# The mixer's values as one block of 1024 columns, with seven products for three of its pairs, and pool's grouped product and all heads behind it

## The chip, the cores and the metric

The kernel runs on one core of a Trainium2 chip. Its time is the device time of one execution in microseconds, as the median of the runs. The engines are named as in the profile: PE (products), PEld (its weight loads), DVE (vector engine), ACT (scalar engine with function tables), POOL, and SP, which issues the DMAs.

## The reference

One layer of an encoder for 256 frames of 2048 channels in f32: a SwiGLU half step, a mixer, cross attention to 256 memory tokens, a second SwiGLU half step, and a last norm. The change lies in the mixer:

```python
h = rms_norm(x, mix_norm[l])
proj = h @ w_in[l]
u, q, k, v, g, a_lr = jnp.split(proj, list(IN_SPLITS), axis=-1)   # 1024, 512, 512, 1024, 1024, 16 columns
y_pool = pool_mixer(u, pool_w[l], pool_scale[l])      # 4 groups: causal means, then a 256 x 256 product each
y_gla = gla_mixer(q, k, v, g, a_lr, ...)              # 4 heads of 128 (q, k) and 256 (v) channels
x = x + jnp.concatenate([y_pool, y_gla], axis=-1) @ w_out[l]
```

In `gla_mixer` each head's scores (256 x 256, causal by chunks of 64 frames, with a decay by channel of k) are multiplied with its values; the result is normed by head and gated with silu(g).

## The kernel before

Everything lies in SBUF with channels on the partitions: `xs` and `ys` hold 16 tiles of 128 channels, each with a high and a low part of 256 frames, which together give nearly f32 precision. Weights stream in one unit of 1 MB after the other. `Stream` holds the units in order: each has a load (a DMA from SP into one of three `raw` buffers), a split into a high part (ACT's cast, `wh`) and a low part (DVE's difference, `wl`), and a function that issues its products. A unit is split two units before its products; `wh` and `wl` have three buffers, so a split waits until PE has read the unit three before it. Operations between the units (`st.op(f, n)`) are put into the stream n units later. A scheduler of the language then settles each engine's own order by its own estimate; an engine then works strictly in that order.

PSUM has four tiles of two banks (`ptile`), which all products share in turn.

The units of the mixer, in order, with the short names used below: two blocks for pool's u (8 units); the low-rank unit; q (4 units); k (k1 to k4); the pool unit (`pool_unit`, 48 products of 256 columns for the four grouped 256 x 256 products, from the pooled inputs that lie in tiles 8 to 15 of `ys`); v (v1 to v8); the gate g (g1 to g8). u, q, k and g are made by `block_a`, with channels on the partitions (32 products a unit, tiles named pa). The values are made by `block_b` as two blocks of 512 columns with frames on the partitions: v1 to v4, then v5 to v8, 24 products of 512 columns a unit (tile pb).

A head goes through these steps: `scores` (ACT's and DVE's factors into a tile QD, named m in the trace; the products pq; DVE's copies into the single tile ST), `attend` (the products po; ACT's square, DVE's copy) and `head_squares` (DVE). For two heads together, `head_norms` adds squares over channels on PE (pn) and takes the root (`rsqrt`: DVE, ACT's square root, DVE, then four diagonal tiles), and `head_scale` spreads the factors over the partitions (PE, ps) and multiplies the heads' tiles on DVE. `ev_g` evicts a gate tile: ACT's copy and DVE's sum, silu, the product with the head's tile, and the split into `ys` tiles 8 to 15, over the pooled inputs. `pool_out` writes pool's results into `ys` tiles 0 to 7.

The heads stood like this: scores of heads 0 and 1 behind v5 and v6, the others behind v8 and g1, `head_norms` behind g1 and g3, `head_scale` behind g2 and g5, each then placed among the products by the scheduler.

Elsewhere the kernel has a cheaper block already, `block_s`: one block of 1024 columns with frames on the partitions, in which chosen units ("sevens") do a 2 x 2 product of blocks with seven products in place of eight, that is 21 instructions in place of 24. A seven needs four sums of `xs` blocks (`Sums.make`: five small DVE operations, then a cast and a difference), a longer split (`split_seven`: three sums of weights into T, high and low parts xh and xl of the weights, and wh and wl of T), four PSUM tiles, and at its end a combination (`combine`) and two joins (`join`) on DVE. The tables `OUT_HOMES` and the like say which tiles lend T, xh and xl their room.

Of the kernel before, what the change touches and what calls it, by code (L numbers as in the profile page):

```python
# [9 lines left out]
AF = mybir.ActivationFunctionType  # L10
# [4 lines left out]
P = 128  # L15
D = 2048
S = 256
# [3 lines left out]
NB = 512  # L21
CH = 64
H = 4
# [76 lines left out]
def build(ctx, tc, I, out):  # L100
    nc = tc.nc
    st = Stream()
# [9 lines left out]
    def open_scope(name, shared=None):  # L112


        def f():
            scope["shared"] = shared or {}
            scope["stack"] = ExitStack()
            scope["pool"] = scope["stack"].enter_context(
                tc.tile_pool(name=name, bufs=1, reuse_waits="tile")
            )  # L120
        return f
# [203 lines left out]
    def block_a(srcs, act, evict, delays=(0, 1)):  # L325

        n_k = 4 * len(srcs)
        held = {}

        def unit(gi):  # L330
            def fn(wh, wl):
                if gi == 0:
                    held["ps"] = [ptile(uid("pa")) for _ in range(2)]
                wh, wl = (w.rearrange("p (k n) -> p k n", n=NB) for w in (wh, wl))
                for kk in range(4):
                    k = 4 * gi + kk
                    last = k == n_k - 1
                    a = act[:, k]
                    for n in range(4):
                        ps = held["ps"][n // 2][:, n % 2, :]  # L340
                        cols = slice(n * P, (n + 1) * P)
                        parts = [(ps, wh[:, kk, cols], a.rearrange("p a b -> p (a b)")),
                                 (ps[:, S:], wl[:, kk, cols], a[:, 0, :])]
                        if last:
                            parts.reverse()
                        for i, (o, w, x) in enumerate(parts):
                            nc.tensor.matmul(  # L347
                                o, w, x, start=k == 0 and i == 0, stop=last and i == 1
                            )
            return fn  # L350

        for gi, src in enumerate(srcs):
            st.unit(src, unit(gi))
        for p in range(2):
            st.op(lambda p=p: evict(p, held["ps"][p]), delays[p])
# [48 lines left out]
    class Sums:  # L404
# [1 line left out]

        def __init__(self, name, act, pairs, over, room):
            self.name, self.act, self.pairs, self.over = name, act, pairs, over  # L410
            self.room, self.where = room, {}

        def make(self, g):
            act, i = self.act, self.pairs.index(g)
            n = 3 if self.over else 4
            if i == 0 or i >= self.room:
                room, tag = (self.room, self.name) if i == 0 else (1, f"{self.name}{i}")
                t = scope["pool"].tile([P, room * 6 * P], F32R, tag=tag, name=uid(tag))
                held = min(len(self.pairs), self.room) if i == 0 else 1
                t = t[:, : held * 2 * n * P].rearrange("p (g a n s) -> p g a n s", a=2, n=n, s=P)  # L420
                self.where.update({i + k: t[:, k] for k in range(held)})
            own = self.where[i]
            a, k = jtile(), slice(2 * g, 2 * g + 2)
            nc.vector.tensor_tensor(
                out=a.rearrange("p (k s) -> p k s", k=2), in0=f32(act[:, k, 0, :]),
                in1=f32(act[:, k, 1, :]), op=ALU.add,
            )

            a = a.rearrange("p (n s) -> p n s", n=4)
            p11, p21, p12, p22 = (a[:, m] for m in range(4))  # L430
            nc.vector.tensor_tensor(out=p11, in0=p11, in1=p21, op=ALU.subtract)
            nc.vector.tensor_tensor(out=p21, in0=p22, in1=p21, op=ALU.subtract)
            nc.vector.scalar_tensor_tensor(
                out=p22, in0=p11, scalar=-1.0, in1=p22, op0=ALU.mult, op1=ALU.subtract
            )
            added = nc.vector.tensor_tensor(out=p12, in0=p12, in1=p22, op=ALU.add)
            split(own[:, 0], own[:, 1], a[:, 4 - n :])
            if self.over:
                split(act[:, 2 * g, 0, P:], act[:, 2 * g, 1, P:], p11)
            return None, added  # L440
# [164 lines left out]
    def block_b(srcs, act, evict, delay=0):  # L605

        n_k = 4 * len(srcs)
        held = {}

        def unit(gi):  # L610
            def fn(wh, wl):
                if gi == 0:
                    held["ps"] = ptile(uid("pb"))
                wh, wl = (w.rearrange("p (k n) -> p k n", n=NB) for w in (wh, wl))
                for kk in range(4):
                    k = 4 * gi + kk
                    for h in range(2):
                        products(held["ps"][:, h, :], act, k, h, wh[:, kk], wl[:, kk],
                                 k == 0, k == n_k - 1)
            return fn  # L620

        for gi, src in enumerate(srcs):
            st.unit(src, unit(gi))
        st.op(lambda: evict(held["ps"]), delay)
# [6 lines left out]
    def wblock(w, n0, k0=0, nk=KT):  # L631

        def src(k):
            return lambda raw: wload(raw.rearrange("p (k n) -> p k n", n=NB), w, k, 4, n0)
        return [src(k0 + k) for k in range(0, nk, 4)]
# [301 lines left out]
    ffn(I["ffn1_w_gate"][0], I["ffn1_w_up"][0], I["ffn1_w_down"][0], down_first,  # L937
        amid_first)
    st.op(close_scope, 1)
    st.op(open_scope("s_mix"), 1)  # L940


    w_in = I["w_in"][0]
# [2 lines left out]
    def mt(name, shape, tag=None, bufs=1):  # L946
        t = whole_lines(scope["pool"], shape, F32, tag or name, uid(name), bufs)
        mix[name] = t
        return t
# [68 lines left out]
    def pool_out(g):  # L1018
        for dt in range(2):
            split_scaled(ys, 2 * g + dt, mix["pp", g][:, dt, :], gcol(G_PS + 2 * g + dt))  # L1020
# [88 lines left out]
    st.op(ev_a)  # L1109
    st.op(decay, 2)  # L1110
    block_a(wblock(w_in, 2 * NB), xs, ev_q)
    block_a(wblock(w_in, 3 * NB), xs, ev_k)
    st.unit(load_pool, pool_unit)
    for g in range(4):
        st.op(lambda g=g: pool_out(g))

    def ev_v(b):
        def evict(ps):
            if b == 0:
                mt("v", [P, 2, 2 * NB])  # L1120
                s = mt("ST", [P, 2, S])
                nc.gpsimd.memset(s[64:128, 0, 0:CH], 0.0)
                nc.gpsimd.memset(s[64:128, 1, 2 * CH : 3 * CH], 0.0)
            for h in range(2):
                nc.scalar.activation(
                    mix["v"][:, h, b * NB : (b + 1) * NB], ps[:, h, :], AF.Copy, scale=Rcol[:, h : h + 1]
                )
        return evict

    def scores(h):  # L1130
        q, kd, E, F = mix["q"][:, h, :], mix["k"][:, h, :], mix["E"], mix["F"]
# [22 lines left out]
            nc.vector.tensor_copy(s[part, j // 2, j * CH :], ps[part, j // 2, j * CH : S])  # L1154

    def attend(h):
        s, v = mix["ST"], mix["v"]
        po = ptile(uid("po"))
        for vt in range(2):
            col = h * DV + vt * P  # L1160
            nc.tensor.matmul(  # L1161
                po[:, vt, :S], v[:, 0, col : col + P], s[:, 0, :], start=True, stop=False
            )
            nc.tensor.matmul(
                po[:, vt, 2 * CH : S], v[:, 1, col : col + P], s[:, 1, 2 * CH :], start=False, stop=True
            )
        if h % 2 == 0:
            mix["oz", h // 2] = as_four(m4())
        q = mix["osq", h] = ttile()
        nc.scalar.activation(q, po[:, :, :S], AF.Square)  # L1170
        i = h % 2
        nc.vector.tensor_copy(mix["oz", h // 2][:, 2 * i : 2 * i + 2, :], po[:, :, :S])

    def head_squares(h):
        sq = mix["osq", h]
        nc.vector.tensor_tensor(out=sq[:, 0, :], in0=sq[:, 0, :], in1=sq[:, 1, :], op=ALU.add)
# [14 lines left out]
    def head_scale(b):  # L1191
        ps = ptile(uid("ps"))
        for i in range(4):
            spread(ps[:, i // 2, :], i % 2, mix["diag"][i])
        for i in range(2):
            oz = mix["oz", b][:, 2 * i : 2 * i + 2, :]
            nc.vector.tensor_tensor(out=oz, in0=oz, in1=bc(ps[:, i, :S]), op=ALU.mult)
# [12 lines left out]
            split_pair(ys, 8 + 2 * h, t)  # L1210
        return evict

    for b in range(2):
        block_b(wblock(w_in, (4 + b) * NB), xs, ev_v(b))
        for i in range(2):
            h = 2 * b + i
            at = 1 + i - b
            st.op(lambda h=h: scores(h), at)
            st.op(lambda h=h: attend(h), at + 1)
            st.op(lambda h=h: head_squares(h), at + 1)  # L1220
        st.op(lambda b=b: head_norms(b), 5 - 2 * b)
        st.op(lambda b=b: head_scale(b), 6 - b)
    block_a(wblock(w_in, 6 * NB), xs, ev_g(0), (0, 0))
    block_a(wblock(w_in, 7 * NB), xs, ev_g(1))
    st.op(close_scope, 1)
# [401 lines left out]
```

## Time and profile before

| | |
|---|---|
| median of 3 runs | 2081.63 us (2081.42 to 2082.89) |
| the profiled execution: its own time | 2082.5 us |
| its span, first to last instruction | 2080.3 us |
| mean granted clock of TensorE | 0.999 |

A matmul's row shows how long it was under way; matmuls overlap, so that the distance of two starts is what one costs. In the rows, x counts instructions, and a bracket at the end of a timeline's row tells how long the engine had been idle and what ended that. Times in the views by time are microseconds from the span's start. f32 products that aren't split (pq, po, pn, ps) appear as two records each.

### The profile page before, as it was taken

How to read it: one execution, taken by the hardware profiler on the slowest of the kernel's cores; microseconds unless marked ns; L12 is line 12 of the kernel's file. 1: busy time of each engine (PE TensorE's matmuls, PEld its weight loads, DVE VectorE, ACT ScalarE, POOL GpSimd, SP SyncE). 2: the span in 40 equal slices, each digit the busy share in tenths (PEclk: the TensorE clock that was granted, in tenths of full speed). 3: DMA queues.
4: the chain of work that ended last, by engine and by line, in shares of the span. 5: the costliest groups of instructions: out<-in, count | busy, mean ns of one | idle time of the engine just before them, and what ended most of it. 6: DMA issues, size and time to landing. Idle time of an engine off the chain costs nothing.

```text
span 2080.3 us, 24347 instructions
## 1 busy us (share of the span) xinstructions
PE 2067.9 (99%) x9651; PEld 1726.1 (83%) x9651; DVE 1800.3 (87%) x1686; ACT 1143.5 (55%) x1136; POOL 98.6 (5%) x87
## 2 busy tenths in 40 slices
PE   9999999999999999999999999999999999999998
PEld 7888888888888888888888888888888888888886
DVE  6998899989998677579889878879988999889987
ACT  7664455544555545455656554656554555545554
POOL 0000000000000000000000000000100010000001
PEclk9999999999999999999999999999999999999999
DMA  7666766566656755557655555666576765676664
GB/s 264 203 202 223 242 216 214 187 229 228 234 194 220 247 180 182 162 182 266 224 180 194 168 182 182 204 221 204 181 243 215 235 209 191 224 241 223 210 226 151
DMA packets 131178, 435.95 MB, mean 210 GB/s; under 512 B 9844, under 2 KB 13528, under 8 KB 130680
## 3 DMA queue, kind: packets, MB, share of 16 engines
q1 hardware_dynamic: 130888, 433.86, 61.9%
q8 instruction: 76, 1.25, 0.2%
q10 hardware_dynamic: 176, 0.53, 0.1%
q14 instruction: 38, 0.31, 0.0%
HBM read 417.58 MB, written 16.78 MB: 209 GB/s over the span
## 4 chain that ended last, share of the span: by engine, by line
PE 99%; DMA 0%; DVE 0%; ACT 0%; SPq 0%; DVEq 0%; issue 0%; ACTq 0%
PE pt L362 58%; PE pt L507 28%; PE pa L347 7%; PE pb L362 2%; PE ph L780 1%; PE pl L1321 1%; PE pv L1358 1%; PE px L791 1%; DMA x<-in_x 0%; PE pp L1012 0%; PE pe L362 0%; PE pa L1039 0%; PE po L1161 0%; PE tm L1268 0%; PE px L717 0%; PE pq L1148 0%
## 5 line engine op out<-in xcount | busy, mean ns | idle before, releaser
L362 PE MATMUL pt<-wh,xs 128*128 128x512 f32 x2080 | 667.5, 390 | 0.0
L453 DVE TENSOR_TENSOR wl<-raw,wh 128x2048 fp32r<-128x2048 f32 (+1 forms) x253 | 545.2, 2161 | 133.2 <-ACT wh L1585 132.9
L1585 ACT CAST wh<-raw 128x2048 fp32r<-128x2048 f32 x253 | 483.2, 1912 | 295.3 <-PE pt L362 134.2
L362 PE MATMUL pt<-wh,ys 128*128 128x512 f32 x1472 | 464.0, 389 | 0.0
L489 ACT CAST wh<-T 128x1024 fp32r<-128x1024 f32 x242 | 254.1, 1055 | 368.5 <-DVE T L486 358.8
L362 PEld LDWEIGHTS pt<-wh,xs 128*128 128x128 f32 x2080 | 389.6, 188 | 80.2 <-ACT wh L1585 0.2
L362 PE MATMUL pt<-wl,xs 128*128 128x512 f32 x1040 | 405.5, 391 | 0.0
L362 PEld LDWEIGHTS pt<-wh,ys 128*128 128x128 f32 x1472 | 276.2, 188 | 57.1
L362 PE MATMUL pt<-wl,ys 128*128 128x512 f32 x736 | 286.9, 390 | 0.0
L453 DVE TENSOR_TENSOR wl<-T,wh 128x2048 fp32r<-128x2048 f32 (+1 forms) x121 | 271.6, 2245 | 2.5 <-ACT wh L489 2.2
L362 PEld LDWEIGHTS pt<-wl,xs 128*128 128x128 f32 x1040 | 195.3, 188 | 39.8
L280 DVE TENSOR_TENSOR xl<-raw,xh 128x1536 fp32r<-128x1536 f32 x121 | 211.9, 1751 | 13.5 <-ACT xh L279 13.4
L279 ACT CAST xh<-raw 128x1536 fp32r<-128x1536 f32 x121 | 179.0, 1480 | 49.8 <-PE pt L507 31.3
L486 DVE TENSOR_TENSOR T<-T,raw 128x512 f32<-128x512 f32 x242 | 167.0, 690 | 6.3
L362 PEld LDWEIGHTS pt<-wl,ys 128*128 128x128 f32 x736 | 138.2, 188 | 28.4
L486 DVE TENSOR_TENSOR T<-raw 128x1024 f32<-128x1024 f32 x121 | 147.4, 1219 | 0.5
L507 PE MATMUL pt<-wh,xs 128*128 128x512 f32 x376 | 146.2, 389 | 0.0
L507 PE MATMUL pt<-xh,xs 128*128 128x512 f32 x376 | 140.3, 389 | 0.0
L457 POOL TENSOR_TENSOR wl<-raw,wh 128x768 fp32r<-128x768 f32 x40 | 74.2, 1856 | 1373.9 <-DVE wl L453 1351.1
L347 PE MATMUL pa<-xs,wh 128*128 128x512 f32 x384 | 135.6, 397 | 0.0
L507 PE MATMUL pt<-wh,xe 128*128 128x512 f32 x320 | 124.4, 389 | 0.0
L347 PE MATMUL pa<-xs,wl 128*128 128x256 f32 x384 | 106.8, 282 | 0.0
(248 smaller groups left out, 2343.9 us busy)
## 6 DMA issues: line engine op xcount, KB each, us to landing
raw<-in_ffn_w_down SPq DMA_DIRECT2D x88, 1024.0 KB, 5.6
raw<-in_ffn_w_up SPq DMA_DIRECT2D x80, 1024.0 KB, 5.0
raw<-in_ffn_w_gate SPq DMA_DIRECT2D x77, 1024.0 KB, 5.1
raw<-in_w_in SPq DMA_DIRECT2D x32, 1024.0 KB, 5.2
raw<-in_xattn_w_kv SPq DMA_DIRECT2D x32, 1024.0 KB, 5.0
raw<-in_w_out SPq DMA_DIRECT2D x16, 1024.0 KB, 5.5
raw<-in_xattn_w_q SPq DMA_DIRECT2D x16, 1024.0 KB, 5.5
raw<-in_xattn_w_o SPq DMA_DIRECT2D x16, 1024.0 KB, 6.0
```

What stands on the lines that cost most here:

```text
L279: in_turn("scalar", lambda: nc.scalar.copy(hi, src))
L280: in_turn("vector", lambda: nc.vector.tensor_tensor(out=lo, in0=src, in1=f32(hi), op=ALU.subtract))
L347: nc.tensor.matmul(o, w, x, start=k == 0 and i == 0, stop=last and i == 1)
L362: nc.tensor.matmul(ps, a, w, start=first and i == 0, stop=last and i == 2)
L453: in_turn("vector", lambda: nc.vector.tensor_tensor(out=lo[:, :n], in0=src[:, :n], in1=f32(hi[:, :n]), op=ALU.subtract))
L457: rest = nc.gpsimd.tensor_tensor(out=lo[:, n:], in0=src[:, n:], in1=f32(hi[:, n:]), op=ALU.subtract)
L486: in_turn("vector", lambda: nc.vector.tensor_tensor(out=o, in0=a, in1=b, op=ALU.add))
L489: in_turn("scalar", lambda: nc.scalar.copy(th[:, c], t[:, c]))
L507: nc.tensor.matmul(banks[n], x, w, start=n in fresh and j == 0, stop=n in ends and j == 2)
L780: nc.tensor.transpose(v[:, i, h * P : (h + 1) * P], g[:, h, i * P : (i + 1) * P], ident)
L791: nc.tensor.transpose(v[:, j, h * P : (h + 1) * P], x[:, h, j * P : (j + 1) * P], ident)
L1585: in_turn("scalar", lambda: nc.scalar.copy(hi, raw))
```

## The change

The values become one `block_s` of 1024 columns: units v1 to v8 load 256 rows of 1024 columns each, and pairs 2, 4 and 6, at places 3, 5 and 7 (v3, v5, v7), are sevens. Their sums (`v_sums`) are made in the k block (put 0, 1 and 2 units behind the q block) and lie in tiles 0 to 5 of `ys`, which are free until `pool_out`; so `Sums` takes places from outside. T, xh and xl get one tile each in the mixer's scope (`MIX_HOMES`; xh and xl have two elsewhere). The values now lie in the tile that the combination writes; ACT scales them there, and `v_part` finds a head's columns. The pool unit and `pool_out` move from behind the k block to behind v8. ST takes the room of the low-rank weights (wa2). All four heads follow the pool unit: scores of head h behind the pool unit and h gate units, `attend` and `head_squares` one unit later, `head_norms` behind g3 and g5, `head_scale` behind g4 and g6. The gate blocks themselves stay as they are.

```diff
-        def __init__(self, name, act, pairs, over, room):
+        def __init__(self, name, act, pairs, over, room, where=None):
             self.name, self.act, self.pairs, self.over = name, act, pairs, over
-            self.room, self.where = room, {}
+            self.room, self.where, self.own = room, where or {}, where is None
...
-            if i == 0 or i >= self.room:
+            if self.own and (i == 0 or i >= self.room):
...
-    st.op(open_scope("s_mix"), 1)
+    MIX_HOMES = {"T": [("T", D, 1)], "xh": [("xh", 3 * NB, 1)], "xl": [("xl", 3 * NB, 1)]}
+    st.op(open_scope("s_mix", MIX_HOMES), 1)
...
     block_a(wblock(w_in, 2 * NB), xs, ev_q)
+    def in_ys(i):
+        t = ys[:, 2 * i : 2 * i + 2].rearrange("p k a s -> p (k a s)")
+        return t.rearrange("p (a n s) -> p a n s", a=2, n=4)
+
+    v_sums = Sums("ve", xs, (2, 4, 6), False, 3, {i: in_ys(i) for i in range(3)})
+    for g, after in zip(v_sums.pairs, (0, 1, 2)):
+        st.op(lambda g=g: among_weights(lambda: v_sums.make(g)), after)
     block_a(wblock(w_in, 3 * NB), xs, ev_k)
-    st.unit(load_pool, pool_unit)
-    for g in range(4):
-        st.op(lambda g=g: pool_out(g))
-
-    def ev_v(b):
-        def evict(ps):
-            if b == 0:
-                mt("v", [P, 2, 2 * NB])
-                s = mt("ST", [P, 2, S])
...
+    def v_home():
+        return mt("v", [P, 4, NB])
+
+    def ev_v(j, c):
+        for h in range(2):
+            nc.scalar.activation(c[:, h, :], c[:, h, :], AF.Copy, scale=Rcol[:, h : h + 1])
+
+    def v_part(t, col):
+        j, at = divmod(col, NB)
+        return mix["v"][:, 2 * (1 - j) + t, at : at + P]
+
+    def score_tile():
+        s = mt("ST", [P, 2, S], "wa2")
...
-    for b in range(2):
-        block_b(wblock(w_in, (4 + b) * NB), xs, ev_v(b))
-        for i in range(2):
-            h = 2 * b + i
-            at = 1 + i - b
-            st.op(lambda h=h: scores(h), at)
-            st.op(lambda h=h: attend(h), at + 1)
-            st.op(lambda h=h: head_squares(h), at + 1)
-        st.op(lambda b=b: head_norms(b), 5 - 2 * b)
-        st.op(lambda b=b: head_scale(b), 6 - b)
+    block_s(wwide(w_in, 4 * NB), xs, v_sums, tuple(range(8)), ev_v, home=v_home)
+    st.unit(load_pool, pool_unit)
+    for g in range(4):
+        st.op(lambda g=g: pool_out(g))
+    st.op(score_tile)
+    for h in range(H):
+        st.op(lambda h=h: scores(h), h)
+        st.op(lambda h=h: attend(h), h + 1)
+        st.op(lambda h=h: head_squares(h), h + 1)
+        if h % 2:
+            st.op(lambda b=h // 2: head_norms(b), h + 2)
+            st.op(lambda b=h // 2: head_scale(b), h + 3)
     block_a(wblock(w_in, 6 * NB), xs, ev_g(0), (0, 0))
     block_a(wblock(w_in, 7 * NB), xs, ev_g(1))
```

More of the change, by code (lines that the diff above doesn't have):

```diff
@@ L1111, in build @@
     block_a(wblock(w_in, 2 * NB), xs, ev_q)
-    block_a(wblock(w_in, 3 * NB), xs, ev_k)
-    st.unit(load_pool, pool_unit)
-    for g in range(4):
-        st.op(lambda g=g: pool_out(g))
-    def ev_v(b):
-        def evict(ps):
-            if b == 0:
-                mt("v", [P, 2, 2 * NB])
-                s = mt("ST", [P, 2, S])
[L1122 to L1128, printed above, removed]
+    def in_ys(i):
[4 more added lines that the diff above has]
+        st.op(lambda g=g: among_weights(lambda: v_sums.make(g)), after)
+    block_a(wblock(w_in, 3 * NB), xs, ev_k)
+    def v_home():
[8 more added lines that the diff above has]
+        s = mt("ST", [P, 2, S], "wa2")
+        nc.gpsimd.memset(s[64:128, 0, 0:CH], 0.0)
+        nc.gpsimd.memset(s[64:128, 1, 2 * CH : 3 * CH], 0.0)
     def scores(h):
@@ L1156, in attend @@
     def attend(h):
-        s, v = mix["ST"], mix["v"]
+        s = mix["ST"]
         po = ptile(uid("po"))
@@ L1161, in attend @@
             nc.tensor.matmul(
-                po[:, vt, :S], v[:, 0, col : col + P], s[:, 0, :], start=True, stop=False
+                po[:, vt, :S], v_part(0, col), s[:, 0, :], start=True, stop=False
             )
             nc.tensor.matmul(
-                po[:, vt, 2 * CH : S], v[:, 1, col : col + P], s[:, 1, 2 * CH :], start=False, stop=True
+                po[:, vt, 2 * CH : S], v_part(1, col), s[:, 1, 2 * CH :], start=False, stop=True
             )
```

## The prediction

> **What bounds the kernel now.** I read the page first, for the share of each engine and the chain that ended last.
>
> ```profile
> span 2080.3 us, 24347 instructions
> PE 2067.9 (99%) x9651; PEld 1726.1 (83%) x9651; DVE 1800.3 (87%) x1686; ACT 1143.5 (55%) x1136; POOL 98.6 (5%) x87
> PE 99%; DMA 0%; DVE 0%; ACT 0%; SPq 0%; DVEq 0%; issue 0%; ACTq 0%
> ```
>
> PE is busy 99% of the span and is the whole chain. A product left out is time saved, and any wait of PE is time lost: there is no cover on that engine. What one product costs is its pitch, not its duration, since products overlap. The views by tile give it:
>
> ```profile
> L1039 PE MATMUL pa<-xs,wh x16: 387/389/398, 755.4 to 758.8; 128*128 128x512 f32 x16
> L362 PE MATMUL pb<-wh,xs x128: 387/389/505, 811.9 to 858.6; 128*128 128x512 f32 x128
> ```
>
> Sixteen products of 512 columns start in 755.4 to 758.8: 3.4 / 15 = 0.227 us each. The next view, busy time by stretch (k2 to the pool unit, then v1 to v8, then g1 to g8; columns PE, PEld, DVE, ACT, POOL, clock, DMA), shows what else is near full:
>
> ```profile
> 789.20:811.90 22.70, 22.70 (x147) 20.45 (x146) 20.00 (x23) 10.69 (x11) 2.82 (x1) 1.00 0.55 188
> 811.90:861.10 49.20, 49.20 (x235) 39.89 (x233) 27.16 (x38) 22.59 (x27) 0.00 (x0) 1.00 0.59 189
> 861.10:913.10 52.00, 52.00 (x315) 45.82 (x314) 35.55 (x60) 24.37 (x26) 0.00 (x0) 1.00 0.45 145
> ```
>
> PE is full in all three. DVE has 2.7 us left in the first and 22 us in the second.
>
> **The products.** v1 to v8 hold 24 products each now; v3, v5 and v7 will hold 21. That is 9 x 0.227 = 2.05 us less on the path, and it is the only saving. Pool's 48 products and the heads' are moved, not changed.
>
> **DVE's added work.** A seven's split on DVE is seen later in the trace, in the output projection:
>
> ```profile
> 926.75 1.22 DVE L486 TENSOR_TENSOR T<-raw 128x1024 f32<-128x1024 f32 x1
> 928.36 1.41 DVE L486 TENSOR_TENSOR T<-T,raw 128x512 f32<-128x512 f32 x2
> 929.68 1.75 DVE L280 TENSOR_TENSOR xl<-raw,xh 128x1536 fp32r<-128x1536 f32 x1
> 931.35 2.28 DVE L453 TENSOR_TENSOR wl<-T,wh 128x2048 fp32r<-128x2048 f32 x1
> ```
>
> Its last row is what an ordinary unit pays too; the other three are extra, 4.4 us, so 13 us for three. The combination and the two joins are 4.6 us (operations of 512 and 1024 columns: 0.6 + 1.14 + 0.6 + 2 x 1.14 by the pitches of those rows). Both lie in v1 to v8, against 22 us of idle, and the heads' work there moves out. Laid out in DVE's new order with these durations, each split is done before its first use: v1's by about 1.5 us, v3's by 3, v5's and v7's by 4. The single xh and xl mean that v5's first cast waits until PE has read v3's (12 of its 21 products); the other 9 and the 24 of v4 leave 33 x 0.227 = 7.5 us for ACT's casts and the 1.75 and 2.28 of xl and wl behind them, which ought to do. I cost this at nothing, hidden behind PE's products; without that cover DVE's 4.4 us per seven are the most it could cost, 13 us in all.
>
> **The sums in the k block** are different. There DVE had 2.7 us left, and the first sum's small operations come ahead of k3's weights:
>
> ```profile
> 789.42 2.28 DVE L453 TENSOR_TENSOR wl<-raw,wh 128x2048 fp32r<-128x2048 f32 x1
> 791.62 1.22 DVE L1075 TENSOR_TENSOR m<-m 128x1024 f32<-128x1024 f32 x1
> 792.76 0.68 DVE L319 TENSOR_TENSOR q<-pa,c 128x512 f32<-128x512 f32 x1
> 793.99 0.68 DVE L1095 SCALAR_TENSOR_TENSOR q<-q,R 128x512 f32<-128x512 f32 x1
> 794.90 1.92 ACT L1585 CAST wh<-raw 128x2048 fp32r<-128x2048 f32 x1 [0.91 <-PE pa L347]
> ```
>
> The 789.42 row is k3's low part; it ended at 791.7. The 794.90 row waits for the end of k2, so k3 starts at 794.8. In the new order the work of 791.62 to 794.6 (3.0 us) and four of the sum's small operations (0.2 us each) come first. The low part then starts near 793.2 and ends at 795.5. PE's new order puts two high products ahead (to 795.3), and the weights must still be loaded: PE waits 0.45 us, between 0 and 0.8.
>
> **The heads behind the pool unit** cost most. Their products need PSUM tiles, of which there are four. Two are held by the first gate block until its eviction, so the heads' tiles and the first tile of the second gate block take turns in the other two. In PE's new order the last products of g4 are followed by pn (heads 0, 1), po of head 2, pq of head 3, ps (heads 0, 1), po of head 3, and only then g5, whose first tile is the one that ps used: it waits for head_scale's two products on DVE. Before, the same operations stood among the products of g1 to g5, so nothing waited long for them. PE's own share, in the chain of waits:
>
> ```profile
> 861.34 5.63 PE pa L347 x32
> ...
> 868.69 0.43 PE po L1161 x2
> 869.12 0.22 PE po L1164 x2
> ...
> 876.36 0.79 PE pq L1148 x6
> ...
> 878.05 0.89 PE ps L233 x8
> ...
> 885.11 0.34 PE pn L1183 x4
> 885.45 5.50 PE pa L347 x31
> ```
>
> po is twice (0.43 + 0.22) = 1.30, pq 0.79, ps 0.89, pn twice 0.34. The cluster is 0.68 + 1.30 + 0.79 + 0.89 + 1.30 = 4.96 us if nothing waits. But head_norms' square root is on ACT behind g4's eviction, g7's cast and a table load. The same sequence, before:
>
> ```profile
> 888.88 1.29 ACT L318 COPY c<-pa 128x512 f32<-128x512 f32 x2 [3.14 <-PE pa L347]
> 890.07 1.91 ACT L1585 CAST wh<-raw 128x2048 fp32r<-128x2048 f32 x1
> 892.00 1.28 ACT L1204 ACT_TABLE_LOAD   x1
> ...
> 870.98 0.53 ACT L1138 COPY m<-q 128x64 f32<-128x64 f32 x3
> 871.52 1.28 ACT L215 ACT_TABLE_LOAD   x1
> 872.82 0.20 ACT L215 ACTIVATE chain<-chain 128x4 f32<-128x4 f32 x1
> ```
>
> Call X the moment at which g4's products are through. Before, the run of 31 from 885.45 held 23 of g4, so X was 885.45 + 23 x 5.50 / 31 = 889.5. From there ACT's row gives copies to X + 0.7, cast to X + 2.5, load to X + 3.8, root to X + 4.0. DVE is strictly in order, and head 3's factors stand behind the reciprocal:
>
> ```profile
> 871.12 0.69 DVE L1172 COPY m<-po 128x512 f32<-128x512 f32 x1
> 871.72 0.41 DVE L1176 TENSOR_TENSOR t<-t 128x256 f32<-128x256 f32 x1
> 873.05 0.18 DVE L216 RECIPROCAL r<-chain 128x4 f32<-128x4 f32 x1
> 873.87 0.88 DVE L228 TENSOR_SCALAR diag<-ident,r 128x128 f32<-128x128 f32 x4
> ...
> 878.85 1.32 DVE L1154 COPY ST<-pq 64x256 f32<-64x256 f32 x4
> 880.21 1.28 DVE L1197 TENSOR_TENSOR m<-m,ps 128x512 f32<-128x512 f32 x2
> ```
>
> Reciprocal and product, X + 4.4; the copy of po waits for ACT's square of it (0.6 behind the root) and runs X + 4.7 to 5.3; the sum of squares to X + 5.7; six factors of 0.165 (871.72 + 0.34 to 873.05) to X + 6.7. pq of head 3 ends at X + 7.3. DVE finishes the diagonals at X + 7.7, copies ST to X + 9.0; po of head 3 ends at X + 10.4, and so does head_scale (X + 10.3). g5 starts at X + 10.4 in place of X + 4.96: PE stands for 5.4 us. Bounds: 4.5 if some order is kinder by a cast's half, 6.4 if each of some ten handovers costs 0.1 us. I take 5.4, since every term has its own row. Behind it g7's low part is late next (DVE's queue brings it at X + 20, PE wants it at X + 22): no further wait.
>
> The heads stand in fewer places, which spares switches between kinds of product. Before, v1 to g8 took 811.9 to about 913.1, 101.2 us; 192 x 0.227 + 8 x 5.63 + 4 x (0.79 + 1.30) + 2 x (0.68 + 0.89) = 100.1. Of the other 1.1 us I give back 0.4 (0 to 1.1).
>
> A rule to weigh on the load: the row has the root 0.02 us behind the 1.28 us load. The Trainium skill's page "ScalarE: Activation LUTs", section "What ACT_TABLE_LOAD costs", adds a drain of about 1.38 us to each switch. By that rule X + 4.0 would be X + 5.4 and the sum 1.4 us more; the row shows the copies' end at 871.51 and the load at 871.52, so the trace has no such drain and the row decides.
>
> **Sum**, against the profiled execution's own 2082.5 us (span 2080.3, 2.2 around it): 2082.5 - 2.05 + 0.45 + 5.4 - 0.4 = 2085.9. The median of the runs, 2081.63, lies 0.87 lower; the forecast is 2081.63 + 3.4 = **2085.0**, its own range 2083.3 to 2086.8. I count 0.2% (4.2 us: 2077.5 to 2085.8) as no change.
>
> **Rivals.** (1) The clock falls in the gap, and the change is slower. Between po of head 2 (X + 2.2) and pq of head 3 (X + 6.3) PE does nothing for 4.1 us. Clock by stretch:
>
> ```profile
> 8.00:10.00 2.00, 0.17 (x3) 0.19 (x3) 0.96 (x2) 1.22 (x5) 0.00 (x0) 1.00 0.96 376
> 2071.00:2074.60 3.60, 0.24 (x2) 0.00 (x0) 2.78 (x9) 2.16 (x7) 0.64 (x1) 1.00 0.56 197
> 2074.60:2080.30 5.70, 0.00 (x0) 0.00 (x0) 1.16 (x3) 0.87 (x2) 0.00 (x0) 0.51 0.57 213
> 1.42 2.82 PE L206 MATMUL pwarm<-ident 128*128 128x128 f32 x12 [1.42 <-POOL ident masks.py:199]
> ```
>
> A gap of about 2 us at the start left the clock at 1.00; the last products ended at 2071.24, and by 2074.6 it was half: 3.4 us of idling suffice. Above 3.4 us it decides. At half rate (0.235 us a piece in the last row, twice ps's 0.11) pq and po take 2.1 us more and g5 begins slow: +2.5, so 2087.5. Against it: one fall is shown, at one phase. The Trainium skill's page "TensorE: Matmul & The Clock Gate", section "Part 1: The HAM clock gate", says that free-running windows of 3413 ns decide; by that a gap of 4.1 holds a whole window in (4.1 - 3.41) / 3.41 = 20% of runs, an estimate from that page. Chance 0.19.
>
> (2) DVE falls behind in k3 to v7. For it: 20.00 of 22.70 busy there, some 7 us of sums added. A split 1.5 us later at two places beyond their slack is +3: 2088. Against it: idle follows in v1 to v8. Chance 0.11.
>
> (3) The gap doesn't come about: the root is there in time, as at 872.82 before. Then 2.05 and 0.4 are saved: 2079.2. For it: the chain of handovers is read off an order, not a run. Against it: g5's tile cannot be had without head_scale. Chance 0.12.
>
> **Numbers.** The forecast has 0.58; a quarter of it, 0.15, lies over 2085.8. Slower: 0.15 + 0.18 of (1) + 0.11 = 0.44. Faster needs more than the products give: 0.02. No change: 0.54. The range 2081.0 to 2088.5 leaves out (3) and the far end of (1) and (2).
>
> **What would show it.** Right: one idle stretch of PE of some 4 us ahead of head 3's pq, ended by DVE's factors, with the root behind a cast and a table load on ACT, and pieces of 1 us ahead of head 3's po and g5; 183 products of 512 columns in the values; k3 starting its low products under 1 us late. Wrong: PE full over g4 and g5 (then 3); clock under 1.00 there (then 1); waits on xl or wl in v1 to v8 (then 2).

## The result and the profile after

| | before | after |
|---|---|---|
| median of 10 runs | 2081.63 us (2081.40 to 2082.89) | 2087.04 us (2085.88 to 2088.44) |
| profiled execution, its span | 2082.5, 2080.3 us | 2087.1, 2085.3 us |
| mean granted clock of TensorE | 0.999 | 0.997 |

The ratio is 1.0025, with a 95% interval of 1.0016 to 1.0033: the changed kernel is 5.4 us slower. By the median that is more than the 0.2% that count as no change here; the interval's lower end, 0.16%, is a little less. The time lies in the range of 2081.0 to 2088.5 and 2.0 us above the forecast of 2085.0.

The changed kernel's page has this line of busy times:

```profile
PE 2069.0 (99%) x9642; PEld 1727.6 (83%) x9642; DVE 1822.0 (87%) x1721; ACT 1150.5 (55%) x1146; POOL 103.7 (5%) x89
```

PE's busy time is 1.1 us more than before, with nine products fewer: some of its work has become slower. The view by stretch (columns PE, PEld, DVE, ACT, POOL, clock, DMA) shows where. The rows are k2's end and k3, k4, v1 to v8, and the stretch from the end of g4's products to the start of g5's:

```profile
788.05:799.96 11.91, 11.82 (x68) 9.94 (x66) 11.77 (x24) 6.31 (x9) 4.37 (x1) 1.00 0.27 89
799.96:806.60 6.64, 5.42 (x31) 4.42 (x30) 6.47 (x9) 2.67 (x3) 0.00 (x0) 1.00 0.47 158
806.60:848.10 41.50, 41.50 (x185) 34.37 (x184) 37.60 (x30) 21.27 (x17) 2.96 (x2) 1.00 0.68 227
...
881.83:893.91 12.08, 8.10 (x42) 7.21 (x40) 7.27 (x27) 4.86 (x9) 0.00 (x0) 0.72 0.03 13
```

PE is full in v1 to v8. In the mixer it waits in two places only: in the k block, where DVE is full (11.77 of 11.91 and 6.47 of 6.64), and between g4 and g5, where no engine is full and the clock is 0.72. v1 to v8 take 41.50 us, which is 183 x 0.227: the sevens work as they should.

**The k block.** PE's timeline at the two waits, and DVE's between them:

```profile
793.57 0.64 PE L347 MATMUL pa<-xs,wh 128*128 128x512 f32 x2
794.30 0.38 PE L347 MATMUL pa<-xs,wl 128*128 128x256 f32 x1
...
799.96 0.63 PE L362 MATMUL pt<-wh,xs 128*128 128x512 f32 x2
801.81 0.39 PE L347 MATMUL pa<-xs,wl 128*128 128x256 f32 x1 [1.23 <-DVE wl L453]
```

```profile
791.96 2.29 DVE L453 TENSOR_TENSOR wl<-raw,wh 128x2048 fp32r<-128x2048 f32 x1
...
796.80 0.68 DVE L286 TENSOR_TENSOR ys<-j,ys 128x512 fp32r<-128x512 f32 x1
...
797.57 0.68 DVE L424 TENSOR_TENSOR j<-xs 128x512 f32<-128x512 f32 x1
...
799.47 2.28 DVE L453 TENSOR_TENSOR wl<-raw,wh 128x2048 fp32r<-128x2048 f32 x1
```

The row at 791.96 is k3's low part and ends at 794.25; PE goes on at 794.30. The row at 799.47 is k4's and ends at 801.75; PE goes on at 801.81. At 0.227 us a product PE was through with the two products ahead at 794.02 and 800.41, so it lost 0.28 us at k3 and 1.40 at k4. Ahead of k4's low part stand the first sum's difference (796.80) and the second sum's five operations (797.57 to 799.47).

**The heads behind g4.** PE's timeline, then ACT's, then DVE's:

```profile
881.83 0.95 PE L1191 MATMUL pn<-ones,t 128*128 128x1 f32 x8
...
888.18 1.30 PE L1156 MATMUL pq<-m,k 128*64 128x256 f32 x5 [3.98 <-DVE m L1148]
...
889.62 2.08 PE L233 MATMUL ps<-diag,ones 128*128 128x128 f32 x8
891.49 1.06 PE L1169 MATMUL po<-ST,v 128*128 128x256 f32 x2
...
893.91 0.55 PE L347 MATMUL pa<-xs,wh 128*128 128x512 f32 x1
```

```profile
881.33 1.29 ACT L318 COPY c<-pa 128x512 f32<-128x512 f32 x2 [1.23 <-PE pa L347]
882.51 1.90 ACT L1595 CAST wh<-raw 128x2048 fp32r<-128x2048 f32 x1
884.43 1.28 ACT L215 ACT_TABLE_LOAD   x1
885.72 0.20 ACT L215 ACTIVATE chain<-chain 128x4 f32<-128x4 f32 x1
```

```profile
885.96 0.18 DVE L216 RECIPROCAL r<-chain 128x4 f32<-128x4 f32 x1 [2.98 <-ACT chain L215]
...
886.45 0.69 DVE L1180 COPY m<-po 128x512 f32<-128x512 f32 x1
...
887.46 0.25 DVE L1148 TENSOR_SCALAR m<-q,E 128x64 f32<-128x64 f32 x1
```

This is the chain of the forecast, link by link: copies, cast, table load, root, reciprocal, the copy of po, then head 3's factors, and only then pq. With X = 881.83 the root starts at X + 3.9 (forecast: done at X + 4.0) and pq at X + 6.35 (forecast: X + 6.5, as pq ends at X + 7.3 and takes 0.79). What comes behind pq is slower than forecast: ps takes 1.87 us (889.62 to 891.49) in place of 0.89, the products po 2.4 (891.49 to 893.91) in place of 1.30. The clock shows why, in stretches of 3.41 us:

```profile
883.82:887.23 3.41, 0.37 (x3) 1.00 0.00 0
887.23:890.64 3.41, 2.46 (x13) 0.50 0.02 5
890.64:894.06 3.42, 3.42 (x14) 0.50 0.00 0
```

From 887.23 to 894.06 the granted clock is half. So the first rival came on top of the forecast. The load begins 0.02 us behind the cast's end and the root 0.01 us behind the load's, so the drain of the Trainium skill's page "ScalarE: Activation LUTs", section "What ACT_TABLE_LOAD costs", is in this trace no more than in the one before.

### The profile page after: what moved, and what is told of

It is laid out like the page before. It is cut to its first block, busy times and chain, and to the rows that moved or that the text cites. A ratio compares the mean times of both kernels' runs of the same rounds, so it can differ in the third digit from the quotient of the medians.

```text
span 2085.3 us, 24379 instructions
## 1 busy us (share of the span) xinstructions
PE 2069.0 (99%) x9642; PEld 1727.6 (83%) x9642; DVE 1822.0 (87%) x1721; ACT 1150.5 (55%) x1146; POOL 103.7 (5%) x89
## 3 DMA queue, kind: packets, MB, share of 16 engines
q8 instruction: 75, 1.23, 0.2%
## 4 chain that ended last, share of the span: by engine, by line
PE 97%; DVE 1%; ACT 1%; DMA 0%; issue 0%; SPq 0%; DVEq 0%; ACTq 0%
PE pt L362 59%; PE pt L507 28%; PE pa L347 5%; PE ph L780 1%; PE pl L1331 1%; PE pv L1368 1%; PE px L791 1%; DVE wl L453 0%; PE pp L1013 0%; PE pe L362 0%; DMA x<-in_x 0%; ACT wh L1595 0%; PE pa L1040 0%; PE tm L1278 0%; PE po L1169 0%; PE ps L233 0%
## 5 line engine op out<-in xcount | busy, mean ns | idle before, releaser
L362 PE MATMUL pt<-wh,xs 128*128 128x512 f32 x2160 | 693.2, 390 | 0.0
L453 DVE TENSOR_TENSOR wl<-raw,wh 128x2048 fp32r<-128x2048 f32 (+1 forms) x250 | 536.3, 2151 | 109.8 <-ACT wh L1595 109.5
L1595 ACT CAST wh<-raw 128x2048 fp32r<-128x2048 f32 x250 | 477.6, 1913 | 272.2 <-PE pt L362 137.1
L362 PEld LDWEIGHTS pt<-wh,xs 128*128 128x128 f32 x2160 | 404.8, 188 | 83.2 <-ACT wh L1595 0.2
L489 ACT CAST wh<-T 128x1024 fp32r<-128x1024 f32 x248 | 260.3, 1054 | 374.7 <-DVE T L486 365.2
L362 PE MATMUL pt<-wl,xs 128*128 128x512 f32 x1080 | 420.9, 390 | 0.0
L453 DVE TENSOR_TENSOR wl<-T,wh 128x2048 fp32r<-128x2048 f32 (+1 forms) x124 | 278.3, 2245 | 2.6 <-ACT wh L489 2.2
L362 PEld LDWEIGHTS pt<-wl,xs 128*128 128x128 f32 x1080 | 203.0, 188 | 41.3
L280 DVE TENSOR_TENSOR xl<-raw,xh 128x1536 fp32r<-128x1536 f32 x124 | 217.1, 1750 | 13.8 <-ACT xh L279 13.7
L279 ACT CAST xh<-raw 128x1536 fp32r<-128x1536 f32 x124 | 183.5, 1480 | 58.0 <-PE pt L507 39.3
L507 PE MATMUL pt<-wh,xs 128*128 128x512 f32 x382 | 148.4, 389 | 0.0
```

What stands on the lines that cost most here:

```text
L279: in_turn("scalar", lambda: nc.scalar.copy(hi, src))
L280: in_turn("vector", lambda: nc.vector.tensor_tensor(out=lo, in0=src, in1=f32(hi), op=ALU.subtract))
L362: nc.tensor.matmul(ps, a, w, start=first and i == 0, stop=last and i == 2)
L453: in_turn("vector", lambda: nc.vector.tensor_tensor(out=lo[:, :n], in0=src[:, :n], in1=f32(hi[:, :n]), op=ALU.subtract))
L489: in_turn("scalar", lambda: nc.scalar.copy(th[:, c], t[:, c]))
L507: nc.tensor.matmul(banks[n], x, w, start=n in fresh and j == 0, stop=n in ends and j == 2)
```

## The experiments

In each only the named edit differs from the changed kernel. "Before" ran beside them on the same chips, with medians of 2081.42 (for the first four) and 2081.19 us. The changed kernel's 2087.04 us is from the first comparison, in which the kernel before had 2081.63, so a difference against it can be off by those 0.2 to 0.4 us.

**Sums made early.** The three sums move from the k block to the u blocks.

```diff
+    for g, after in zip(v_sums.pairs, (3, 6, 7)):
+        st.op(lambda g=g: among_weights(lambda: v_sums.make(g)), after)
     block_a(wblock(w_in, 0), xs, ev_pool(0))
...
     block_a(wblock(w_in, 2 * NB), xs, ev_q)
-    for g, after in zip(v_sums.pairs, (0, 1, 2)):
-        st.op(lambda g=g: among_weights(lambda: v_sums.make(g)), after)
```

> Only the place of v_sums differs from the changed kernel: they are made in the u blocks (3, 6 and 7 units behind the start of the first), where DVE is idle 2.5 to 3.3 us in each unit, and not in the k block. Theory (the sums ahead of k3's and k4's low parts cost the two waits of PE at 794.30 and 801.81, 0.3 and 1.4 us): both waits go, nothing new comes in the u blocks, the heads' gap stays as it is; 2087.0 - 1.8 = 2085.3 us, 2084.9 to 2085.7. Rival (DVE is full over k and v in any case, so that its lateness moves to v1 to v7): waits on low parts of 1 us or more appear there, 2086.5 to 2087.2.

2085.26 us (2084.64 to 2088.59, 11 runs), 1.78 less than the changed kernel. DVE's timeline in the k block:

```profile
788.82 2.28 DVE L453 TENSOR_TENSOR wl<-raw,wh 128x2048 fp32r<-128x2048 f32 x1
...
796.30 2.28 DVE L453 TENSOR_TENSOR wl<-raw,wh 128x2048 fp32r<-128x2048 f32 x1
```

By the traces' own times k3's and k4's low parts come 3.1 and 3.2 us earlier than in the changed kernel (791.96, 799.47), and PE has no wait left in the k block, nor in u, q or v. From u's first product to the end of g4 PE takes 173.10 us in this trace (707.61 to 880.71) and 174.87 in the changed kernel's (706.96 to 881.83), 1.77 less. The two waits were the sums' doing and were worth 1.8 us.

**All heads one unit earlier.** Every step of every head, from scores of head 0 (now behind v8) on.

```diff
+    st.op(score_tile)
+    for h in range(H):
+        st.op(lambda h=h: scores(h), h)
...
     st.unit(load_pool, pool_unit)
...
-    st.op(score_tile)
-    for h in range(H):
-        st.op(lambda h=h: scores(h), h)
...
```

> Only the heads differ from the changed kernel: every step of every head stands one unit earlier (scores of head 0 behind v8, and so on), so that g4's 32 products lie between the products pn of heads 0 and 1 and the later heads. Theory (the gap is the chain cast, table load, root, reciprocal, head 3's factors, with no gate products left to cover it): the idle stretch of 4 us and the fall of the clock go, some new short waits of 0 to 1.5 us in all; 2087.0 - 7.1 + 0 to 1.5 = 2079.9 to 2081.4 us, clock 0.999. Rival (four PSUM tiles are too few for all heads behind the pool unit, wherever they stand): the wait moves to another place of g1 to g5 with its length, 2085 or more.

2089.31 us (2088.58 to 2089.66, 5 runs): slower still, as the rival said. The wait behind g4 is gone, but a longer one has come behind the pool unit. PE's and DVE's timelines there:

```profile
862.40 1.09 PE L1156 MATMUL pq<-m,k 128*64 128x256 f32 x2 [5.67 <-DVE m L1148]
```

```profile
857.76 2.29 DVE L453 TENSOR_TENSOR wl<-raw,wh 128x2048 fp32r<-128x2048 f32 x1 [1.30 <-ACT wh L1595]
859.97 0.87 DVE L240 SCALAR_TENSOR_TENSOR ys<-pp,gains,ys 128x256 fp32r<-128x256 f32 x2
860.75 0.68 DVE L1180 COPY m<-po 128x512 f32<-128x512 f32 x1
...
861.68 0.25 DVE L1148 TENSOR_SCALAR m<-q,E 128x64 f32<-128x64 f32 x1
```

PE's order puts pq of head 1 ahead of g1's products. Its factors (861.68) stand on DVE behind a weight split, pool's outputs and the copy of po, as head 3's stood behind the reciprocal. The granted clock falls here too, to half from 859.00 to 865.83. My reason for this kernel, that g4's products would cover the root, held for the root; it was not the root that bound in the new place. But the rival's own reason, too few PSUM tiles, isn't shown either: PE waits for factors here, not for a tile.

**The gap filled.** 36 spare products (transposes into the unused half of pn's tile) run where PE idles.

```diff
+    def spare(n):
+        for _ in range(n):
+            nc.tensor.transpose(mix["pn"][:, 1, :P], ident, ident)
...
+        if h == 2:
+            st.op(lambda: spare(36), h + 1)
```

> The changed kernel with 36 spare transposes of 128 columns (some 3.9 us) on PE behind the products po of head 2, into the unused half of pn's tile, which nobody reads: PE is busy through most of the gap, and every wait of the heads stays. Theory (the clock falls because PE is idle, and the half rate costs 1.7 us on top of the chain): clock 0.999, g5 starts 10.4 us behind g4's products in place of 12.1, 2085.3 us (2084.9 to 2085.8). Rival (what is slow behind the gap is DVE's order and not the clock): 2087.0 again, with the clock up. Third case: the spare products themselves delay head 3's, 2087.5 or more.

2085.38 us (2084.59 to 2085.92, 11 runs), 1.66 less than the changed kernel. PE's timeline, and a row of the view by stretch (clock behind the bracketed counts):

```profile
881.88 0.95 PE L1191 MATMUL pn<-ones,t 128*128 128x1 f32 x8
...
884.08 4.09 PE L1201 MATMUL pn<-ident 128*128 128x128 f32 x36
...
892.27 0.47 PE L347 MATMUL pa<-xs,wh 128*128 128x512 f32 x1
```

```profile
887.00:890.00 3.00, 2.94 (x27) 2.50 (x25) 2.95 (x16) 0.00 (x0) 0.00 (x0) 1.00 0.00 0
```

With the clock up, g5 starts at 892.27 - 881.88 = 10.39 us behind g4's products: the X + 10.4 of the forecast. Without the filling it was 893.91 - 881.83 = 12.08. The 1.7 us between them are the clock's price, and adding work made the kernel faster. In the changed kernel's trace the clock was low for two stretches of 3.41 us; in the traces with early sums and without sevens it was low for one, and there g5 starts 11.30 and 11.10 us behind g4's products. So the price is 0.7 to 1.7 us, by how long the clock stays low.

**No sevens.** Eight units of 24 products; no sums, no combination (ACT writes the values into their tile straight from the products); pool and heads as in the change.

```diff
-    block_s(wwide(w_in, 4 * NB), xs, v_sums, tuple(range(8)), ev_v, home=v_home)
+    block_t(wwide(w_in, 4 * NB), xs, ev_v)
```

> The changed kernel with the values as one block of 1024 columns but 24 products in all eight units: no seven, no sums, no combination; pool and heads in the changed order. Theory (nine products are 2.05 us, the sums' waits 1.8 us, both go; the heads' gap belongs to their order alone and stays with 12 us and the low clock): 2087.0 + 2.05 - 1.8 = 2087.3 us, and 2.05 us above the kernel with early sums. Rival (DVE's three long splits take back the nine products somewhere in v1 to v8): as fast as the kernel with early sums or faster, 2085.3 or less. Rival (the sevens' load on DVE is what makes the heads late): the gap shrinks by 2 us or more, 2085 or less.

2087.16 us (2086.18 to 2089.06, 8 runs), 1.90 above the kernel with early sums: the nine products' 2.05 us, within the scatter. In the traces PE takes 175.14 us from u's first product to the end of g4 (707.15 to 882.29), 2.04 more than with early sums. PE waits 4.0 us for pq behind g4 here too, and the clock falls. So the gap belongs to the order of pool and heads, not to the sevens' load on DVE.

**The table load moved away.** A root of one column brings the table, 14 us ahead of head_norms' own root (871.56 in place of 885.72).

```diff
+    def root_table():
+        nc.scalar.activation(mix["spare"][:, 0:1], mix["osq", 0][:, 0, 0:1], AF.Sqrt)
...
+    st.op(root_table, 2)
```

> The changed kernel with one more root of a single column on ACT, of head 0's squares and into a tile that nobody reads, so that ACT loads the root's table some 10 us earlier, where it is idle; head_norms' own root then finds its table. Theory (cast, load, root, reciprocal and factors are one chain, each link worth its duration): root 1.3 us earlier, head 3's scores start 5.1 us behind g4's products in place of 6.35; if the clock falls all the same 2087.0 - 1.3 = 2085.7 us, if it stays 2084.0; which of the two is open, since 2.7 us of PE's idling are left. Rival (the factors wait for another thing than the root, the copy of po or a PSUM tile): no change, 2087.0.

2084.65 us (2084.05 to 2086.45, 11 runs). ACT's and PE's timelines:

```profile
870.26 1.28 ACT L1208 ACT_TABLE_LOAD   x1
...
882.44 1.90 ACT L1600 CAST wh<-raw 128x2048 fp32r<-128x2048 f32 x1
884.24 0.21 ACT L215 ACTIVATE chain<-chain 128x4 f32<-128x4 f32 x1
```

```profile
881.76 0.95 PE L1191 MATMUL pn<-ones,t 128*128 128x1 f32 x8
...
886.70 0.89 PE L1156 MATMUL pq<-m,k 128*64 128x256 f32 x6 [2.58 <-DVE m L1148]
```

The root follows the cast at once, and pq starts at X + 4.94 in place of X + 6.35: 1.4 us, the load and its handovers. In the traced run, of 2084.26 us, the clock stays up, and ps takes its ordinary time. Five of the eleven runs have a mean clock of 0.999 and take 2084.05 to 2084.61; six have 0.998 or 0.997 and take 2084.65 to 2086.45. So both foreseen times, 2084.0 and 2085.7, lie in what occurs, but the slower runs are spread and form no second group.

**Factors made early.** `scores` is cut in two: `factors_of` makes QD on ACT and DVE, `scores` keeps the products pq and the copies into ST.

```diff
-    def scores(h):
+    def factors_of(h):
...
+    def scores(h):
+        q, kd, QD = mix["q"][:, h, :], mix["k"][:, h, :], mix["QD", h]
...
+    for h in range(2):
+        st.op(lambda h=h: factors_of(h))
...
+        if h < 2:
+            st.op(lambda h=h: factors_of(h + 2), h + 1)
```

> The changed kernel with scores cut in two: the factors (ACT's and DVE's, into the tile QD) of heads 0 and 1 are made behind the pool unit and those of heads 2 and 3 one unit earlier than now; products, copies, norms and everything else keep their places, and the sums stay in the k block. Theory (head 3's factors behind the reciprocal on DVE are what holds PE): PE's order then puts gate products between the heads' ones, the idle stretch of 4 us and the low clock go, some 0.7 to 1.5 us of waits are left, 2087.0 - 7.1 + 0.7 to 1.5 = 2080.6 to 2081.4 us, clock 0.999. Rival (the root itself binds: head_scale's products need it, and g5 needs their tile): the wait moves from pq to ps and is 2 to 3 us long, 2082.5 to 2083.5 or more.

2082.79 us (2082.43 to 2086.02, 11 runs): 4.25 less than the changed kernel, 1.4 more than expected at most. Behind g4 it did what the theory said: pq of head 3 follows 11 gate products without a wait, the clock stays at 1.00, and PE waits about 0.6 us (ps begins at 886.37 and takes 0.89, po follows at 887.90), for the copies into ST. But PE's timeline has a new wait in the k block, and DVE's shows its cause:

```profile
797.16 0.39 PE L347 MATMUL pa<-xs,wl 128*128 128x256 f32 x1 [2.86 <-DVE wl L453]
```

```profile
791.84 0.58 DVE L1148 TENSOR_SCALAR m<-q,E 128x64 f32<-128x64 f32 x3
...
792.53 2.37 DVE L1089 TENSOR_TENSOR F<-F,E 128x4 f32<-128x4 f32 x1
794.83 2.28 DVE L453 TENSOR_TENSOR wl<-raw,wh 128x2048 fp32r<-128x2048 f32 x1
```

The first factors need only q and E. The scheduler put three of a second head (791.84) into the k block ahead of k3's low part, beside the sums, and with them the decay's products F (792.53), which in the changed kernel came behind it, at 794.16. The low part came at 794.83 in place of 791.96, and PE's one idle stretch of 2.86 us there replaces the 0.09 and 1.23 of the changed kernel. I had said that only the heads' places would change.

**Both, and the last head's steps later.** Early sums, early factors; `attend` of head 3 behind g5, norms and scale of heads 2 and 3 behind g6 and g7.

```diff
+    for g, after in zip(v_sums.pairs, (3, 6, 7)):
...
+    st.op(lambda: attend(3), 5)
+    st.op(lambda: head_norms(1), 6)
+    st.op(lambda: head_scale(1), 7)
```

> Early sums (as in the kernel that moves the sums to the u blocks) and early factors together, and besides attend of head 3 behind g5, head_norms of heads 2 and 3 behind g6 and their head_scale behind g7, each one unit later than in the changed kernel. Theory (with both waits gone nothing but the nine products and a few switches is left of the change): 2081.4 - 2.05 - 0.4 to 1.1 = 2078.3 to 2079.0 us, clock 0.999, no wait of PE over 0.3 us in the mixer. Rival (a wait of 1 us or more comes anew, at head 3's products among g5 or at the last gates behind the later norms): 2080 to 2082.

2079.00 us (2077.99 to 2081.32, 11 runs); against before the ratio is 0.9990, with an interval of 0.9981 to 0.9999. It beats both kernels. The chain of waits, in order of time (start, length, what):

```profile
880.02 2.94 PE pa L347 x17
882.96 0.80 PE pq L1160 x6
883.76 1.09 PE ps L233 x8
884.85 5.85 PE pa L347 x33
```

It is PE alone, and no wait of PE is left in the mixer: gate products stand between the heads' steps. From u's first product to the output projection's first one PE takes 202.79 us (707.42 to 910.21), and 204.93 before (708.21 to 913.14). These 2.14 us are the nine products (2.05 by the pitch) and little else.

**A third of the filling.** 12 spare products in place of 36.

> As the kernel with the gap filled, but 12 spare transposes in place of 36: 1.3 us of work behind po of head 2, so that PE idles some 2.7 us in place of 4. It tells how much idling lowers the clock. If a stretch of 3.4 us without any work is needed, the clock stays up in every run: clock 0.999, 2085.4 us. If less suffices, it falls in some or all runs (0.998 or 0.997), and the time lies between 2085.4 and 2087.0.

2086.51 us (2085.01 to 2087.54, 11 runs), near the upper end: the traced run fell to half clock after an idle stretch of 2.68 us, so 3.4 us without any work are not needed. Three of the eleven runs have a mean clock of 0.999.

## Why the prediction was right, and where not

- **The products.** 2.05 us forecast; 1.90 by the medians, 2.04 by the traces up to the end of g4, between the two kernels that differ in the sevens and their sums alone, both without waits in k.
- **The splits in v1 to v8.** Costed at nothing, and rightly: PE is full there, though DVE was fuller (37.60 of 41.50 us) than the 22 us of idle in the old stretch suggested.
- **The sums.** This term was mis-sized: 0.45 us forecast, 1.78 measured. The place was right for k3, whose wait was 0.28 us; 1.40 came at k4. I had followed DVE's queue to k3's low part and no further; k4's has a whole second sum ahead of it. The five operations that a sum puts ahead of a low part, each of which waits for the one before it, take 1.90 us (797.57 to 799.47), where four of 0.2 had been counted, ahead of k3 alone. The second rival, DVE falling behind, so came true in part: at one place in k, and nowhere in v1 to v8.
- **The heads.** 5.4 us forecast; with the clock held up, 10.39 - 4.96 = 5.43. The chain's order was right, and its links are shown singly: without the load it shrinks by about the load, without the factors behind the reciprocal the wait all but goes. One reason given isn't seen: g5 does not wait for the tile of ps. In the changed kernel's trace head_scale is through at 893.01 and g5 starts at 893.91, right behind po of head 3.
- **The clock.** Here the prediction failed: "Above 3.4 us it decides" and the 20% of runs taken from a window that must be empty. A window with 0.37 us of work in it was enough. The clock fell in all three traces with the full gap (the changed kernel, early sums, no sevens). Six of the ten runs of the changed kernel have a mean clock of 0.997, which none of the 57 runs of the kernel before that ran beside the experiments has; the other four have 0.998, which 17 of those 57 have too, so that these four show nothing by themselves. The price was up to 1.7 us, not 2.5: against the kernel with the gap filled pq takes 0.55 us longer and po 1.0, but ps only 0.14, since at full rate PE waits 0.59 us behind it for DVE's copies into ST.
- **The sum.** With the two terms at their measured size it is 2085.0 + 1.3 (sums) + 1.7 (clock) = 2088.0; 2087.04 was measured. The traces place most of the difference. From u's first product to the output projection's first one PE took 204.93 us before and 211.15 after (706.96 to 918.11), 6.22 more. Of that the heads' cluster is 7.12 (12.08 in place of 4.96) and the sums 1.77; less 2.05 for the products, 0.62 is left, which the fewer switches may have saved; 0.4 had been counted for them. Behind the mixer both traces take 1158.10 us to the last product. The rest lies at the start: in the trace of before PE waits 1.83 us for x and u begins at 708.21, in the nine other traces u begins at 706.66 to 707.61. How much of this is in the medians, which differ by 5.4, stays open.

The likeliest single case, no change, was therefore not what came; the text had given 0.44 to slower. The third rival, that the gap doesn't come about, is what the kernel with both corrections makes true: 2.05 + 0.4 = 2.45 us less than before was forecast for it, 2.19 measured. That 2079.2 and 2079.0 lie so close is in part luck, as the kernel before ran 0.44 us faster beside this one.

## What to carry to other kernels

Where one engine is the whole span, follow each in-order queue past the first late operation to the next one that the bound engine needs: the larger wait was at the second. A change that regroups small dependent steps pays by what stands ahead of them in their engines' queues, and moving the whole group a unit earlier only changes what that is; taking out the part that depends on nothing late, here the factors, removes the wait, if its new place has room: in the full k block it made a wait of 2.9 us. And price a gap on TensorE with the clock: behind a gap of 2.68 us the clock fell here, and half rate makes what follows the gap dearer too.

## What the runs showed of the hardware

The clock needs no empty stretch to fall. Every low period in the traces of the mixer lasts 3.41 or 6.83 us, so the clock is decided in windows of 3.41 us. The falls of one trace lie a whole number of such windows apart: with early sums the clock falls at 888.33 and, at the end of the span, at 2076.16, which is 348 x 3.4133. So each trace has a grid of windows, and its place differs: counted back, a window begins 0.86 us behind the span's start in that trace, and 3.18 us in the changed kernel's. These are the windows around the gaps on that grid (PE's busy time and, farther right, the granted clock), for the kernels with early sums (its last row is the window in which the span's last products end), with the load moved away (where no low period shows the grid, it is counted back from the fall at the span's end) and with a third of the filling:

```profile
881.50:884.92 3.42, 1.57 (x10) 1.27 (x9) 0.24 (x2) 3.39 (x4) 0.00 (x0) 1.00 0.00 0
884.92:888.33 3.41, 1.27 (x11) 1.08 (x12) 3.23 (x17) 0.79 (x4) 0.00 (x0) 1.00 0.00 0
888.33:891.74 3.41, 3.41 (x13) 2.84 (x13) 3.14 (x8) 0.00 (x0) 0.00 (x0) 0.50 0.02 5
...
2072.75:2076.16 3.41, 1.44 (x7) 0.86 (x5) 2.35 (x6) 2.76 (x9) 1.83 (x2) 1.00 0.32 115
```

```profile
882.67:886.08 3.41, 1.45 (x9) 1.16 (x8) 1.61 (x7) 2.69 (x6) 0.00 (x0) 1.00 0.00 0
886.08:889.50 3.42, 2.21 (x17) 1.82 (x18) 3.31 (x16) 0.00 (x0) 0.00 (x0) 1.00 0.02 5
```

```profile
884.49:887.91 3.42, 0.74 (x7) 0.54 (x6) 2.21 (x11) 1.94 (x6) 0.00 (x0) 1.00 0.00 0
887.91:891.33 3.42, 3.42 (x17) 3.12 (x17) 2.55 (x12) 0.00 (x0) 0.00 (x0) 0.50 0.02 5
```

The clock was halved behind windows in which PE was busy for 0.37 (the changed kernel, above), 0.74, 1.27 and 1.44 us, and stayed behind windows of 1.45 and 1.57. So the traces sort themselves at some 42% of a window. The nearest two, 1.44 and 1.45, are closer than busy times can be trusted, since the ends of products are modelled in the profile, and no run set the share on purpose. The Trainium skill's page "TensorE: Matmul & The Clock Gate", section "Part 1: The HAM clock gate", has the window's length, 3413 ns, and that it runs freely, and the trace agrees with both; it asks for an idle window before the clock falls, and there the measurements differ, so they decide. For the rise, a window with 2.46 us of work at half rate (887.23 to 890.64 of the changed kernel) was not enough, one that was full was. The start of the kernel, where the clock is low at first, narrows this: with both corrections four transposes (px) at 4.35 take 0.66 us, behind a window with 2.77 us of work (0.79 to 4.20), but with early factors the same four at 4.40 take 1.11 us, behind one with 2.48 (0.50 to 3.91). And the spare transposes counted as work: behind a window filled with them the clock stayed at 1.00.
